# Two-layer hybrid trunk on one core: matmuls of one contraction depth issued together, exponentials one group ahead of their transposes, first weights on two queues

## The chip, the core and the metric

The kernel runs on one core of a Trainium2 chip. The core has five engines that run side by side and meet through semaphores: TensorE (PE, matmuls and transposes), VectorE (DVE), ScalarE (ACT, functions and casts), GpSimd (POOL) and SyncE (SP, which here issues DMAs). The time is that of the device in microseconds (us) for one execution; lower is better.

## What is computed

The reference is a trunk of two layers over 512 tokens of 1024 features, in float32. Each layer is a mixer, a residual layer norm, a convolutional FFN and a second residual layer norm:

```python
for layer in range(DEPTH):                    # DEPTH = 2
    mix = even_mixer(h, ...) if layer % 2 == 0 else odd_mixer(h, ...)
    h = layer_norm(DEEPNORM_ALPHA * h + mix, ...)
    ffn = conv_ffn(h, ...)
    h = layer_norm(DEEPNORM_ALPHA * h + ffn, ...)

def even_mixer(x, ...):                       # x @ w_in, split
    o_a = gated_delta_rule(q_a, k_a, v_a, g, beta)   # 6 heads of 128
    o_a = rms_norm(o_a, norm_w) * silu(z_a)
    o_b = dilated_attention(q_b, k_b, v_b, rel_bias) # 3 groups x 4 heads of 64
    return concatenate([o_a, o_b]) @ w_out

def dilated_branch(q, k, v, window, dilation, rel_bias):  # once per group
    s = where(mask, q . k * dh ** -0.5 + bias, -inf)      # blocks of 128 queries
    m = max(s); p = exp(s - m); l = sum(p)
    return (p / l) @ v, m + log(l)            # groups are joined by softmax over these
...
def gla_chunked(q, k, v, log_a):              # odd mixer, 4 heads, key 64, value 128
    o_n = (q_n * exp(b_n)) @ state + attn @ v_n
    state = exp(b_last) * state + (k_n * exp(b_last - b_n)).T @ v_n
```

The odd mixer joins differential attention (4 heads) with this gated linear attention (GLA).

## The kernel before

Activations lie as features by tokens: 8 tiles `h` of 128 x 512 for the trunk. The large products take float32 operands apart into a rounded part and a remainder (`xh` and `xl` of the activations, `wh` and `wl` of the weights), and each 128 x 128 block of weights becomes three products of 128 x 512 (`xh,wh`, `xl,wh`, `xh,wl`). A unit of weights is a tile `wr` of 128 x 1024 (512 KB, DMA from SP), cast to `wh` on ACT, with the remainder `wl` taken on DVE; one unit gives one output tile `pd` of 24 products. The small products of the mixers run in plain float32; in the trace each of these has two records.

The order on PE is written by a planner in the program. Every part of a mixer is a generator (a `Chain`), and `tile_of` polls the chains after each three products of a unit. A chain that yields `FREE` may go on as soon as PE has done its last piece, one that yields 0 waits for the estimated end plus a hop. So small products land between the products of a unit at places that the estimates set.

`swa_pair` does the dilated attention for a pair of heads, in two calls. For each of three groups g and both heads hh, the four blocks n of 128 queries give scores `sps` (group 0: 128-row products through `scores`; groups 1 and 2: plain products of 64 rows, since a head has 64 features), DVE adds the bias and takes the maxima (`mx`). The maxima are joined over the groups (`combine` into `mrow`), transposed into `pmx`, negated into `negm`, and 24 exponentials follow on ACT with sums `ls`. Then, group by group, PE transposes the exponentials (`pt`), DVE and ACT copy them out, and value products of 64 columns gather in `po`. While this runs, the units of the gate z of the gated delta rule (GDN) pass through PE; their tiles `pd` get a silu on ACT (`zs` or `h`). The GDN means (`pm`) get a logarithm and an exponential on ACT. `out_proj` ends the mixer.

`gla_pair` does two GLA heads. The output tile `po` of a head takes four 128-row products of the chunk's own attention (`vt,ga`) and three 64-row products with the state (`gs,qe`), which alternate.

At the start `START` names the order of the first loads: pieces of the trunk `x` (issued on SP) and of the first two weight units (issued on ACT, the first narrow unit feeds the gates, tile `pa`). ACT casts and DVE subtracts in the same order. `par` and `con` are tables of parameters and constants. `gates` computes the decay of GDN in a chain over ACT and DVE that ends in a scan; `pg` is PE's transpose behind it.

Of the kernel before, what the change touches and what calls it, by code (L numbers as in the profile page):

```python
# [9 lines left out]
F32 = mybir.dt.float32  # L10
# [3 lines left out]
ALU = mybir.AluOpType  # L14
# [3 lines left out]
P = 128  # L18
S = 512
# [5 lines left out]
NCH = S // P  # L25
# [9 lines left out]
_NP = 0  # L35
# [23 lines left out]
for _n, _w in (("ident", 128), ("maskT", 128), ("nm1", 32), ("i32", 32), ("lm", 4 * 32), ("scan", 512),  # L59
# [30 lines left out]
EVEN_SEQ = "h0 h1 h2 h3 h4 h5 q00 v0 q01 v1 q02 v2 q10 q11 q12 z0 z1 z2 z3 z4 z5"  # L90
ODD_SEQ = "0D12G3abcd"

START = (("x", 0, 1), (0, 0, 4), ("x", 1, 2), (1, 0, 2), ("x", 2, 3), (1, 2, 5), ("x", 3, 4), (0, 4, 8), ("x", 4, 5),
         ("x", 5, 6), (1, 5, 8), ("x", 6, 7), ("x", 7, 8))
WARM = 8
LEAD = 3
AHEAD = 2
# [14 lines left out]
FREE = -1  # L112
# [53 lines left out]
class Scratch:  # L166


    def __init__(self, t, pool, n, more=None):
        self.t, self.pool, self.free, self.of = t, pool, list(range(n)), {}  # L170
        if more is not None:
            self.free += [(k, more) for k in range(more.shape[1])]

# [21 lines left out]
class Trunk:  # L195
# [14 lines left out]
    def setup(self):  # L210
        nc, tc, ctx = self.nc, self.tc, self.ctx
# [9 lines left out]

        self.ones = keep.tile([P, P], F32, name="ones")
        nc.gpsimd.memset(self.ones, 1.0 / P)
        idle = keep.tile([P, 1], F32, name="idle")
        tc.keep_in_program_order(nc.scalar.copy(out=idle, in_=self.ones[:, 0:1]))
        for what, a, e in START:
            if what == "x":
                nc.sync.dma_start(self.h[:, a, :], self.xt[:, a, :])
            else:

                u, w = first[what]
                n = 64 if u in NARROW else P
                tc.keep_in_program_order(nc.scalar.dma_start(w[0][:, a * n : e * n], self.wts[u][:, a * n : e * n]))
        self.par = keep.tile([P, _NP], F32, name="par")
        self.con = keep.tile([P, _NCC], F32, name="con")

        warm = self.sps("warm")
# [4 lines left out]
        self.onesP, self.onesK = (keep.tile([P, P], F32R, name=f"ones{i}") for i in "PK")  # L242
        for x, n in ((self.onesP, P), (self.onesK, 512)):
            nc.vector.tensor_scalar(out=x, in0=self.ones, scalar1=P / n, scalar2=None, op0=ALU.mult)
        self.cst = keep.tile([P, 3], F32, name="cst")
        self.one, self.lneps, self.gdneps = (self.cst[:, i : i + 1] for i in range(3))
        nc.gpsimd.memset(self.one, 1.0)
        nc.gpsimd.memset(self.lneps, LN_EPS)
# [503 lines left out]
    def even(self):  # L752
# [8 lines left out]
        def t1(n, w, bufs):  # L761
            return mp.tile([P, w], F32, name=self.nm(n), tag=n, bufs=bufs)

        self.enter(EVEN)
        g = {"zero": t1("zero", 1, 1)}
        seq = EVEN_SEQ.split()
# [480 lines left out]
    def swa_pair(self, pair, taken, vts, bg, o, mp, t1):  # L1247
# [12 lines left out]
        for g in range(3):  # L1260
            while len(taken) < 2 * g + 2 or X.room() < 5 or not self.bias:
                yield None
            q, k = taken[2 * g : 2 * g + 2]
            for hh in range(2):
                r = slice(64 * hh, 64 * hh + 64)
                hd = 2 * pair + hh
                tiles = []
                for n in range(NCH):
                    w = 256 if g == 0 and n > 0 else P
                    if n == 0 or (g == 0 and n == 2):  # L1270
                        while X.room() < 1:
                            yield None
                        x = X.get("sc")
                        held.append(x)
                        off = 0
                    dst = x[:, off : off + w]
                    off += w
                    bias = bg[0][:, hd, 256 - w : 256] if g == 0 else bg[g][:, hd, :]
                    k0 = n * P + P - w
                    ps = self.sps("sps")  # L1280
                    if g == 0:
                        m = max(0, 256 - w)
                        self.scores(ps[:, : w + m], q, k, hh, slice(n * P, (n + 1) * P), slice(k0, k0 + w + m))
                    else:
                        T.matmul(ps[:, :w], lhsT=q[r, n * P : (n + 1) * P], rhs=k[r, k0 : k0 + w], start=True, stop=True)
                    ci = hh * 12 + g * NCH + n
                    V.tensor_tensor_reduce(out=dst, in0=ps[:, :w], in1=bias, scale=0.125, scalar=-3e38,
                                           op0=ALU.add, op1=ALU.max, accum_out=mx[:, ci : ci + 1])
                    tiles.append((dst, k0, w))
                    yield FREE  # L1290
                sc[g, hh] = tiles
            X.put(*(q + k[0] + k[1] if g == 0 else [q, k]))

        def rows(cols, rw):

            pr = self.sps("rows")
            T.transpose(out=pr[0:24, 0:P], in_=cols, identity=self.ident)
            tr = t1("tr", P, 2)
            V.tensor_copy(out=tr[0:24, :], in_=pr[0:24, 0:P])
            for hh in range(2):  # L1300
                G.dma_start(rw[hh : hh + 1, :], tr[12 * hh : 12 * hh + 12, :])
            yield 2500
# [11 lines left out]
        combine(rw, ALU.max, mrow)  # L1314
        yield 0
        pm = self.sps("pmx")
        for g in range(3):
            for n in range(NCH):
                src = perm(mrow[0:2, :])[:, n, :] if g else mrow[0:2, n * P : (n + 1) * P]
                T.transpose(out=pm[:, (g * NCH + n) * 2 : (g * NCH + n) * 2 + 2], in_=src, identity=self.ident[0:2, 0:2])  # L1320
        X.put(mrow)
        nm = t1("negm", 24, 2)
        V.tensor_scalar(out=nm, in0=pm[:, 0:24], scalar1=-1.0, scalar2=None, op0=ALU.mult)
        ls = t1("ls", 24, 2)
        for g in range(3):
            for hh in range(2):
                for n in range(NCH):
                    ci = (g * NCH + n) * 2 + hh
                    li = hh * 12 + g * NCH + n
                    dst, k0, w = sc[g, hh][n]  # L1330
                    A.activation(out=dst, in_=dst, func=AF.Exp, bias=nm[:, ci : ci + 1], accum_out=ls[:, li : li + 1])
                yield 0 if g == 0 and hh == 1 else FREE
        po = self.sps("po")
        for g in range(3):
            while len(vts[g]) < 2:
                yield None
            pts = {}
# [19 lines left out]
            for n in range(NCH):  # L1357
                for i in range(len(pts[0, n])):
                    for hh in range(2):
# [4 lines left out]
                        else:  # L1364
# [1 line left out]
                        vt, f = (vts[g][pair], kb * P) if g else (vts[g][kb // 2], kb % 2 * HS + P * pair)  # L1366
                        T.matmul(dst, lhsT=vt[:, f + 64 * hh : f + 64 * hh + 64], rhs=src,
                                 start=(g == 0 and n == 0 and i == 0), stop=(g == 2 and n == NCH - 1))
                yield FREE
            X.put(*temps)  # L1370
        X.put(*held)
        if pair:
# [172 lines left out]
    def gla_pair(self, pr, cs, qk, vts, gm, o, t1, done):  # L1545
# [4 lines left out]
        def ch(x, n):  # L1550
            return x[:, n * P : (n + 1) * P]
# [100 lines left out]
        vt = vts["G"]  # L1652
# [15 lines left out]
        yield 0  # L1668
        for hh in range(2):
            po = self.sps("po")  # L1670
            for n in range(NCH):
                if n:
                    T.matmul(ch(po, n), lhsT=qe[rr[hh], n * P : (n + 1) * P], rhs=sts[n][rr[hh]], start=True, stop=False)
                T.matmul(ch(po, n), lhsT=ch(ats[hh], n), rhs=ch(vt[n], 2 * pr + hh), start=(n == 0), stop=True)
            ss = t1("gss", NCH, 4)
            for n in range(NCH):
                A.activation(out=ch(ats[hh], n), in_=ch(po, n), func=AF.Square, accum_out=ss[:, n : n + 1])
            yield 0
            yield from self.norm_out(po, ss, o, 4 + 2 * pr + hh, self.p("lnorm"), t1)
            done.append(2 * pr + hh)  # L1680
# [322 lines left out]
```

## Time and profile before

| | |
|---|---|
| median of 3 runs | 1410.34 us (1410.32 to 1410.57) |
| the profiled execution | 1412.89 us |
| its span | 1411.1 us |
| granted PE clock over the span | 0.996 of full |
| PE busy | 1385.7 us, 98% |
| DVE, ACT, POOL busy | 839.3, 673.5, 179.8 us |
| stretches of the span | start to 18 us; even mixer to 374; out_proj and norm to 440 |

The profiled execution took 1.79 us beyond its span and lies 2.55 us above the median. PE has work in nearly all of the span, so a change counts by what it does to PE's own time or to the few waits of PE. A busy PE isn't a PE at its peak: matmuls are pipelined, and the length of a record overlaps with the next. What one product costs is therefore read from the start of one record to the start of the next.

### The profile page before, as it was taken

What the parts mean: (1) busy time and instruction counts of PE and PEld (TensorE: products, weight loads), DVE (VectorE), ACT (ScalarE), POOL (GpSimd) and SP (SyncE); (2) the same over time, 40 slices, a digit from 0 to 9 for tenths busy, and PEclk for the clock granted to TensorE, in tenths of its full rate; (3) what the DMA queues carried; (4) which work ended last, traced back from release to release, by engine and by line L of the source; (5) the groups of instructions that cost most, each with busy time, mean ns of one, the idle gap of its engine ahead of it and who ended that gap; (6) DMA issues with size and microseconds to landing.
All of it is one profiled execution on the core that took longest, in us unless ns stands there. A gap on an engine that the chain in (4) does not pass through costs nothing.

```text
span 1411.1 us, 22721 instructions
## 1 busy us (share of the span) xinstructions
PE 1385.7 (98%) x9050; PEld 1151.2 (82%) x9050; DVE 839.3 (59%) x1635; ACT 673.5 (48%) x1285; POOL 179.8 (13%) x237
## 2 busy tenths in 40 slices
PE   8999999999999999999999999999999999999997
PEld 6878787777798888888888977878898888888886
DVE  6876744544586555555243797777776555553354
ACT  6644433644857344434132755557565344432133
POOL 2103012011023111111010310000131111110010
PEclk9999999999999999999999999999999999999998
DMA  7434112121342322323233313211303322223221
GB/s 248 144 111 149 47 61 75 36 73 61 98 128 76 99 95 97 98 95 100 96 98 98 88 61 105 75 46 60 120 31 119 99 96 95 99 95 100 91 73 60
DMA packets 41457, 130.42 MB, mean 92 GB/s; under 512 B 4637, under 2 KB 9485, under 8 KB 41352
## 3 DMA queue, kind: packets, MB, share of 16 engines
q1 hardware_dynamic: 35584, 119.05, 26.1%
q10 hardware_dynamic: 4184, 4.92, 1.2%
q0 software_dynamic: 1584, 5.00, 1.1%
q8 instruction: 71, 1.16, 0.3%
q14 instruction: 34, 0.28, 0.1%
HBM read 126.76 MB, written 5.29 MB: 94 GB/s over the span
## 4 chain that ended last, share of the span: by engine, by line
PE 83%; DVE 6%; ACT 5%; DMA 3%; issue 2%; POOL 1%; ACTq 0%; DVEq 0%; POOLq 0%
PE pd L487 18%; PE pd L488 18%; PE pd L489 17%; PE pd L371 16%; PE pd L397 3%; DMA wr<-wts 2%; PE pc L159 1%; PE po L159 1%; PE sps L159 1%; PE pz L159 1%; PE py L159 1%; PE pa L159 1%; PE dsc L159 1%; DVE wl L159 1%; PE dpo L159 1%
## 5 line engine op out<-in xcount | busy, mean ns | idle before, releaser
L500 DVE TENSOR_TENSOR wl<-wr,wh 128x1024 fp32r<-128x1024 f32 (+1 forms) x153 | 187.9, 1229 | 301.8 <-ACT wh L499 298.7
L488 PE MATMUL pd<-xl,wh 128*128 128x512 f32 (+1 forms) x968 | 353.6, 366 | 0.2 <-DVE xl L684 0.2
L487 PE MATMUL pd<-xh,wh 128*128 128x512 f32 (+1 forms) x968 | 353.1, 366 | 0.4 <-ACT xh L683 0.4
L489 PE MATMUL pd<-xh,wl 128*128 128x512 f32 (+1 forms) x968 | 353.1, 365 | 0.0
L499 ACT CAST wh<-wr 128x1024 fp32r<-128x1024 f32 (+1 forms) x156 | 159.8, 1030 | 196.7 <-PE pd L488 171.4
L487 PEld LDWEIGHTS pd<-xh,wh 128*128 128x128 f32 x968 | 182.4, 189 | 30.4 <-ACT xh L683 0.9
L488 PEld LDWEIGHTS pd<-xl,wh 128*128 128x128 f32 x968 | 182.6, 189 | 30.1 <-DVE xl L684 1.1
L489 PEld LDWEIGHTS pd<-xh,wl 128*128 128x128 f32 x968 | 182.7, 189 | 29.5 <-issue 0.8
L371 PE MATMUL pd<-xh,wh 128*128 128x512 f32 x424 | 172.7, 407 | 0.0
L371 PE MATMUL pd<-xl,wh 128*128 128x512 f32 x424 | 170.9, 403 | 0.0
L487 PE MATMUL pd<-ah,wh 128*128 128x512 f32 (+1 forms) x396 | 145.1, 366 | 0.0
L489 PE MATMUL pd<-ah,wl 128*128 128x512 f32 (+1 forms) x396 | 144.7, 366 | 0.0
L488 PE MATMUL pd<-al,wh 128*128 128x512 f32 (+1 forms) x396 | 144.7, 365 | 0.0
L721 DVE SCALAR_TENSOR_TENSOR y<-pd,par,y 128x510 f32<-128x510 f32 (+1 forms) x176 | 130.4, 745 | 2.8
L371 PE MATMUL pd<-xh,wl 128*128 128x512 f32 x424 | 117.8, 402 | 0.0
L730 POOL TENSOR_TENSOR al<-y,ah 128x512 fp32r<-128x512 f32 x44 | 59.1, 1343 | 407.6 <-ACT ah L729 407.6
L159 DVE TENSOR_TENSOR wl<-wr,wh 128x1024 fp32r<-128x1024 f32 x63 | 77.1, 1224 | 42.6 <-PE pd L371 17.6
L159 ACT CAST wh<-wr 128x1024 fp32r<-128x1024 f32 x63 | 65.9, 1047 | 66.6 <-PE pd L371 48.2
L371 PEld LDWEIGHTS pd<-xl,wh 128*128 128x128 f32 x424 | 80.5, 190 | 16.2 <-issue 1.9
L371 PEld LDWEIGHTS pd<-xh,wh 128*128 128x128 f32 x424 | 80.4, 190 | 15.7 <-issue 0.3
L371 PEld LDWEIGHTS pd<-xh,wl 128*128 128x128 f32 x424 | 76.4, 188 | 14.6 <-issue 0.7
L487 PEld LDWEIGHTS pd<-ah,wh 128*128 128x128 f32 x396 | 74.7, 189 | 12.2
(387 smaller groups left out, 1868.6 us busy)
## 6 DMA issues: line engine op xcount, KB each, us to landing
wr<-wts SPq DMA_DIRECT2D x213, 512.0 KB, 3.4
h<-xt SPq DMA_DIRECT2D x16, 256.0 KB, 4.1
rep<-tab POOLq DMA_DIRECT2D x1, 3072.0 KB, 15.5
h<-gd POOLq DMA_DIRECT2D x6, 256.0 KB, 7.5
qe<-ge ACTq DMA_DIRECT2D x5, 256.0 KB, 4.4
bd<-rep ACTq DMA_DIRECT2D x1, 1024.0 KB
out<-h SPq DMA_DIRECT2D x2, 512.0 KB, 3.2
con<-con SPq DMA_DIRECT2D x1, 544.0 KB
```

Source lines behind the costliest of these rows:

```text
L159: r = fn(*a, **k)
L371: self.nc.tensor.matmul(ps, lhsT=w[part][:, k * P : (k + 1) * P], rhs=x[:, k, :], start=(i == 0), stop=(i == 23))
L397: self.nc.tensor.matmul(pss[b][:, a : a + n], lhsT=chunk(x[:, k, :], c), rhs=ws, start=(k == 0 and a == 0 and not part and x is self.xh), ...
L487: nc.tensor.matmul(ps, lhsT=wh, rhs=ah, start=first, stop=False)
L488: nc.tensor.matmul(ps, lhsT=wh, rhs=al, start=False, stop=False)
L489: nc.tensor.matmul(ps, lhsT=wl, rhs=ah, start=False, stop=last)
L499: A.copy(out=hi, in_=raw)
L500: V.tensor_tensor(out=lo, in0=raw, in1=hi.bitcast(F32), op=ALU.subtract)
L721: V.scalar_tensor_tensor(out=y[:, sft:], in0=ps[:, : S - sft], scalar=w(2 - sft), in1=y[:, sft:], op0=ALU.mult, op1=ALU.add)
L730: G.tensor_tensor(out=al[:, f, :], in0=y, in1=ah[:, f, :].bitcast(F32), op=ALU.subtract)
```

## The change

It has six parts. Scores of groups 1 and 2 take one tile `ps4` for four products, issued together. Only the maxima of two groups are transposed, since groups 1 and 2 share one maximum (`pmx` 8 products a pair in place of 12). The exponentials become a generator `exps(g)`: group g+1 is issued ahead of the transposes of group g, where before all three groups came ahead of all transposes. The value products of a group are issued without a yield between the blocks. GLA's three state products come ahead of the four others. `START` cuts the first weights into other pieces, of which three are issued on ACT and three on SP, between the pieces of x. Tiles are placed or widened so that all start at multiples of 128 bytes.

```diff
-START = (("x", 0, 1), (0, 0, 4), ("x", 1, 2), (1, 0, 2), ("x", 2, 3), (1, 2, 5), ("x", 3, 4), (0, 4, 8), ("x", 4, 5),
-         ("x", 5, 6), (1, 5, 8), ("x", 6, 7), ("x", 7, 8))
+START = (("x", 0, 1), (0, 0, 2), ("x", 1, 2), (1, 0, 2), ("x", 2, 3), (0, 2, 5), ("x", 3, 4), (1, 2, 5), ("x", 4, 5),
+         (0, 5, 8), ("x", 5, 6), (1, 5, 8), ("x", 6, 7), ("x", 7, 8))
+FIRST = 3
...
+        for i in range(n):
+            pool.tile([P, S], F32, name=t.nm("x"), tag=f"x{i}", bufs=1)
...
-        for what, a, e in START:
+        for i, (what, a, e) in enumerate(START):
...
-                tc.keep_in_program_order(nc.scalar.dma_start(w[0][:, a * n : e * n], self.wts[u][:, a * n : e * n]))
-        self.par = keep.tile([P, _NP], F32, name="par")
+                here = i < 2 * FIRST
+                d = (nc.scalar if here else nc.sync).dma_start(w[0][:, a * n : e * n], self.wts[u][:, a * n : e * n])
+                if here:
+                    tc.keep_in_program_order(d)
+        self.par = keep.tile([P, -(-_NP // 32) * 32], F32, name="par")[:, :_NP]
...
+                if g:
+
+                    ps4 = self.sps("sps")
+                    for n in range(NCH):
+                        b = slice(n * P, (n + 1) * P)
+                        T.matmul(ps4[:, b], lhsT=q[r, b], rhs=k[r, b], start=True, stop=True)
                 for n in range(NCH):
...
-                        T.matmul(ps[:, :w], lhsT=q[r, n * P : (n + 1) * P], rhs=k[r, k0 : k0 + w], start=True, stop=True)
+                        ps = ps4[:, n * P : (n + 1) * P]
...
-        for g in range(3):
+        for g in range(2):
             for n in range(NCH):
                 src = perm(mrow[0:2, :])[:, n, :] if g else mrow[0:2, n * P : (n + 1) * P]
...
-        for g in range(3):
+
+        def exps(g):
             for hh in range(2):
                 for n in range(NCH):
-                    ci = (g * NCH + n) * 2 + hh
+                    ci = (min(g, 1) * NCH + n) * 2 + hh
...
+        yield from exps(0)
         po = self.sps("po")
         for g in range(3):
+            if g < 2:
+                yield from exps(g + 1)
...
-                yield FREE
+            yield FREE
             X.put(*temps)
...
+            for n in range(1, NCH):
+                T.matmul(ch(po, n), lhsT=qe[rr[hh], n * P : (n + 1) * P], rhs=sts[n][rr[hh]], start=(n == 1), stop=False)
             for n in range(NCH):
-                if n:
-                    T.matmul(ch(po, n), lhsT=qe[rr[hh], n * P : (n + 1) * P], rhs=sts[n][rr[hh]], start=True, stop=False)
-                T.matmul(ch(po, n), lhsT=ch(ats[hh], n), rhs=ch(vt[n], 2 * pr + hh), start=(n == 0), stop=True)
+                T.matmul(ch(po, n), lhsT=ch(ats[hh], n), rhs=ch(vt[n], 2 * pr + hh), start=False, stop=(n == NCH - 1))
```

The first list is PE in `swa_pair` of pair 1 before the change, from group 1 on (`sps` scores, `sq` queries and keys, `pd` a unit of the gate z).

```order
L159 MATMUL sps_3832<-sq_3586,sq_3512 128x128
L371 MATMUL pd_3825<-xl,wh_3666 128x512
L159 MATMUL sps_3835<-sq_3586,sq_3512 128x128
L371 MATMUL pd_3825<-xh,wh_3666 128x512
L159 MATMUL sps_3838<-sq_3586,sq_3512 128x128
L159 MATMUL sps_3841<-sq_3586,sq_3512 128x128
L159 MATMUL sps_3846<-sq_3586,sq_3512 128x128
L371 MATMUL pd_3825<-xl,wh_3666 128x512
L159 MATMUL sps_3852<-sq_3586,sq_3512 128x128
L159 MATMUL sps_3855<-sq_3586,sq_3512 128x128
L159 MATMUL sps_3858<-sq_3586,sq_3512 128x128
L371 MATMUL pd_3825<-xh,wh_3666 128x512
```

And PE at the same place with the change:

```order
L160 MATMUL sps_3893<-sq_3589,sq_3545 128x128 x4
L378 MATMUL pd_3832<-xh,wl_3690 128x512 x3
L160 MATMUL sps_3906<-sq_3589,sq_3545 128x128 x4
L160 MATMUL sps_3916<-sq_3754,sq_3682 128x128 x4
L378 MATMUL pd_3832<-xh,wl_3690 128x512 x3
L160 MATMUL sps_3930<-sq_3754,sq_3682 128x128 x4
L160 MATMUL pm_3940<-hi_3617,onesP 128x512
```

The eight score products of group 1 stood in runs of one to three with single weight products between; now the sixteen of groups 1 and 2 stand in runs of four, eight and four, with three weight products between two runs.

The next list is PE in `gla_pair`, first head, before (`dpo` is differential attention, `vt,ga` the chunk's attention, `gs,qe` the state).

```order
L159 MATMUL dpo_8817<-vt_8234,dat_8784 128x128
L159 MATMUL po_8824<-vt_8770,ga_7582 128x128
L159 MATMUL po_8824<-gs_8798,qe_7974 128x128
L159 MATMUL po_8824<-vt_8774,ga_7582 128x128
L159 MATMUL po_8824<-gs_8800,qe_7974 128x128
L159 MATMUL po_8824<-vt_8778,ga_7582 128x128
L159 MATMUL po_8824<-gs_8802,qe_7974 128x128
L159 MATMUL po_8824<-vt_8789,ga_7582 128x128
```

And with the change:

```order
L160 MATMUL dpo_8874<-vt_8291,dat_8841 128x128
L160 MATMUL po_8881<-gs_8855,qe_8031 128x128
L160 MATMUL po_8881<-gs_8857,qe_8031 128x128
L160 MATMUL po_8881<-gs_8859,qe_8031 128x128
L160 MATMUL po_8881<-vt_8827,ga_7639 128x128
L160 MATMUL po_8881<-vt_8831,ga_7639 128x128
L160 MATMUL po_8881<-vt_8835,ga_7639 128x128
L160 MATMUL po_8881<-vt_8846,ga_7639 128x128
```

The two kinds alternated from product to product; now the three state products stand together, ahead of the four others.

The last lists are ACT at the end of the even mixer, pair 1 (`sc` the scores of groups 1 and 2 that get their exponential, `pt` transposed exponentials, `zs` and `h<-pd` the silu of gate z), first before.

```order
L159 ACTIVATE sc_3831,ls_3994<-sc_3831,negm_3992 128x128 x4
L159 ACTIVATE sc_3845,ls_3994<-sc_3845,negm_3992 128x128 x4
L159 ACTIVATE sc_3861,ls_3994<-sc_3861,negm_3992 128x128 x4
L159 ACTIVATE sc_3877,ls_3994<-sc_3877,negm_3992 128x128 x4
L159 COPY pt_4080<-pt_4075 128x512
L159 COPY pt_4087<-pt_4083 128x384
L159 ACT_TABLE_LOAD
L159 ACTIVATE h<-pd_3971 128x512
L159 ACTIVATE h<-pd_4082 128x512
L159 ACTIVATE zs_4143<-pd_4118 128x512
L159 COPY h<-pt_4165 128x512
L159 COPY h<-pt_4187 128x512
```

And with the change, from the copies on:

```order
L160 COPY pt_4113<-pt_4108 128x512
L160 COPY pt_4123<-pt_4119 128x384
L160 ACT_TABLE_LOAD
L160 ACTIVATE zs_4118<-pd_4065 128x512
L160 ACT_TABLE_LOAD
L160 ACTIVATE sc_3921,ls_4045<-sc_3921,negm_4043 128x128 x4
L160 ACTIVATE sc_3935,ls_4045<-sc_3935,negm_4043 128x128 x4
L160 COPY h<-pt_4171 128x512
L160 ACT_TABLE_LOAD
L160 ACTIVATE h<-pd_4127 128x512
L160 COPY h<-pt_4202 128x512
L420 ACT_TABLE_LOAD
```

All sixteen exponentials of groups 1 and 2 stood together ahead of the copies; now the last eight stand behind the copies of group 0 and a silu, with a load of ACT's function table on either side.

## Rows read from the trace of the kernel before

**Rows 1.** Page of the profile, part 1: busy time, share of the span, instructions.

```profile
PE 1385.7 (98%) x9050; PEld 1151.2 (82%) x9050; DVE 839.3 (59%) x1635; ACT 673.5 (48%) x1285; POOL 179.8 (13%) x237
```

**Rows 2.** List of waits, PE: us in total, times, longest.

```profile
PE pg L159 <- ACT wh L159: 1.5, 1, 1.5
...
PE po L159 <- ACT pt L159: 1.3, 1, 1.3
```

**Rows 3.** Timeline of PE, plain weight products; columns: start, length, line, operation, count.

```profile
21.54 1.98 PE L371 MATMUL pd<-xh,wl 128*128 128x512 f32 x8
23.36 0.39 PE L371 MATMUL pd<-xh,wh 128*128 128x512 f32 x1
```

**Rows 4.** Timeline of PE, scores of pair 0, group 2; two records are one product.

```profile
242.73 0.48 PE L159 MATMUL sps<-sq,sq 64*128 64x128 f32 x2
243.15 1.20 PE L371 MATMUL pd<-xh,wl 128*128 128x512 f32 x4
244.28 0.48 PE L159 MATMUL sps<-sq,sq 64*128 64x128 f32 x2
```

**Rows 5.** Timeline of PE, scores of pair 0, group 1.

```profile
204.44 1.36 PE L159 MATMUL sps<-sq,sq 64*128 64x128 f32 x10
205.74 0.50 PE L371 MATMUL pd<-xl,wh 128*128 128x512 f32 x1
```

**Rows 6.** Timeline of PE, value and state products of one GLA head.

```profile
925.97 1.16 PE L159 MATMUL dpo<-vt,dat 128*128 128x128 f32 x8
926.97 0.39 PE L159 MATMUL po<-vt,ga 128*128 128x128 f32 x2
927.28 0.48 PE L159 MATMUL po<-gs,qe 64*128 64x128 f32 x2
...
929.37 0.71 PE L159 MATMUL po<-vt,ga 128*128 128x128 f32 x4
```

**Rows 7.** Timeline of PE, transposes of the maxima of pair 1.

```profile
346.77 1.36 PE L159 MATMUL pmx<-con,mrow 2*128 2x2 f32 x12
```

**Rows 8.** Timeline of ACT and of its DMA queue, start of the kernel.

```profile
4.01 1.36 ACTq L233 DMA_DIRECT2D wr<-wts  x2
5.42 0.62 ACT L257 CAST xh<-h 128x512 fp32r<-128x512 f32 x1 [3.19 <-DMA h<-xt]
```

**Rows 9.** Timeline of PE, first weight products.

```profile
7.16 0.79 PE L507 MATMUL pd<-xh,wh 128*128 128x512 f32 x1 [2.37 <-DVE wh L500]
```

**Rows 10.** Timeline of ACT, weight unit ahead of the gates.

```profile
17.30 1.05 ACT L159 CAST wh<-wr 128x1024 fp32r<-128x1024 f32 x1 [1.14 <-DMA wr<-wts]
```

**Rows 11.** Timeline of DVE, end of the gates' chain.

```profile
28.02 1.21 DVE L159 TENSOR_TENSOR_SCAN h<-con,h 6x512 f32<-6x512 f32 x1
```

**Rows 12.** Table by window, all engines; busy us (count), PEclk, DMA share, GB/s.

```profile
29.00:35.00 6.00, 5.66 (x20) 4.57 (x21) 3.77 (x8) 2.54 (x5) 3.25 (x6) 0.72 0.37 103
```

**Rows 13.** Timeline of ACT, end of the even mixer.

```profile
348.39 0.40 ACT L159 ACTIVATE h<-h,negm 128x128 f32<-128x128 f32 x1 [0.97 <-DVE negm L159]
...
352.71 1.28 ACT L413 ACT_TABLE_LOAD   x1
354.01 0.72 ACT L159 ACTIVATE dt<-dt,cst 128x512 f32<-128x512 f32 x1
...
360.83 0.39 ACT L159 ACTIVATE sc<-sc,negm 128x128 f32<-128x128 f32 x1
...
367.95 1.28 ACT L159 ACT_TABLE_LOAD   x1
...
373.26 2.18 ACT L683 CAST xh<-o 128x512 fp32r<-128x512 f32 x4
```

**Rows 14.** Timeline of PE, mean of GDN pair and first product of out_proj.

```profile
335.73 0.50 PE L159 MATMUL pm<-hi,onesP 128*128 128x512 f32 x1
...
373.93 0.50 PE L487 MATMUL pd<-xh,wh 128*128 128x512 f32 x1 [0.41 <-ACT xh L683]
```

More of the change, by code (lines that the diff above doesn't have):

```diff
@@ L223, in setup @@
         nc.gpsimd.memset(self.ones, 1.0 / P)
-        idle = keep.tile([P, 1], F32, name="idle")
-        tc.keep_in_program_order(nc.scalar.copy(out=idle, in_=self.ones[:, 0:1]))
-        for what, a, e in START:
+        self.cst = keep.tile([P, 32], F32, name="cst")
+        tc.keep_in_program_order(nc.scalar.copy(out=self.cst[:, 8:9], in_=self.ones[:, 0:1]))
+        for i, (what, a, e) in enumerate(START):
             if what == "x":
@@ L244, in setup @@
             nc.vector.tensor_scalar(out=x, in0=self.ones, scalar1=P / n, scalar2=None, op0=ALU.mult)
-        self.cst = keep.tile([P, 3], F32, name="cst")
         self.one, self.lneps, self.gdneps = (self.cst[:, i : i + 1] for i in range(3))
@@ L762, in t1 @@
             return mp.tile([P, w], F32, name=self.nm(n), tag=n, bufs=bufs)
+        for i in range(4):
+            t1(f"st{i}", P, 2)
         self.enter(EVEN)
@@ L1279, in swa_pair @@
                     k0 = n * P + P - w
-                    ps = self.sps("sps")
                     if g == 0:
+                        ps = self.sps("sps")
                         m = max(0, 256 - w)
@@ L1297, in rows @@
             T.transpose(out=pr[0:24, 0:P], in_=cols, identity=self.ident)
-            tr = t1("tr", P, 2)
+            tr = t1("tr", P, 1)
             V.tensor_copy(out=tr[0:24, :], in_=pr[0:24, 0:P])
@@ L1321, in swa_pair @@
         X.put(mrow)
-        nm = t1("negm", 24, 2)
-        V.tensor_scalar(out=nm, in0=pm[:, 0:24], scalar1=-1.0, scalar2=None, op0=ALU.mult)
+        nm = t1("negm", 16, 2)
+        V.tensor_scalar(out=nm, in0=pm[:, 0:16], scalar1=-1.0, scalar2=None, op0=ALU.mult)
         ls = t1("ls", 24, 2)
-        for g in range(3):
+        def exps(g):
             for hh in range(2):
                 for n in range(NCH):
-                    ci = (g * NCH + n) * 2 + hh
+                    ci = (min(g, 1) * NCH + n) * 2 + hh
                     li = hh * 12 + g * NCH + n
```

## The prediction

> **What bounds the kernel now.** I read the page's busy times first: PE is busy for 1385.7 us, 98% of the span [rows 1]. All that PE waits is 25 us, so a gain has to come from PE's own time or from one of its few long waits. The list of waits comes next. Two of them lie near the change: 1.5 us ahead of `pg`, behind the gates' chain, and 1.3 us ahead of `po`, behind ACT's copy `pt` at the end of the even mixer [rows 2]. Then the timeline of PE, where I read starts, not lengths: eight plain weight products start 23.36 - 21.54 = 1.82 us apart, 0.2275 each [rows 3]. That is the price of a product with nothing around it. FFN and out_proj run at that price, have no small products among them and are touched by none of the six parts.
>
> The small products cost more than their own time. Around a score of 64 rows, 242.73 to 244.28 is 1.55 us for one score and four weight products [rows 4]. The four would take 0.91. Five scores in a row, with the way out, take 205.74 - 204.44 = 1.30, or 0.26 each, some 0.22 without the way out [rows 5]. So a lone score brings 1.55 - 0.91 - 0.22 = 0.42 us that is neither work nor a wait: PE goes to another contraction depth and back. GLA shows it without weight products or another engine: six products that alternate between 128 and 64 rows start 929.37 - 926.97 = 2.40 apart, 0.40 each, while four of one depth just ahead take 926.97 - 925.97 = 1.00, 0.25 each [rows 6]. A turn is thus 0.15 to 0.21, a visit (there and back) 0.3 to 0.42.
>
> **Scores, maxima and values on PE.** Score visits fall from 15 to 5 by the order of the whole program, products unchanged: 10 x 0.42 = 4.2 less. Of the transposes of maxima 8 go (4 in each pair) at 1.36 / 12 = 0.11 [rows 7]: 0.9 less. Visits for value products fall from 11 to 8; no row prices these alone, so 0 to 3 x 0.42 = 1.3. Against that, the new order puts single transposes between weight products where before they stood in fours. Going through both orders pair of neighbours by pair of neighbours with the intervals of the rows gives 4.8 less up to out_proj, where the simple sum says 5.1 to 6.4. I take 4.8.
>
> **GLA.** Visits of state products fall from 12 to 4: 8 x 0.3 to 0.42 is 2.4 to 3.4; the neighbours give 3.5, since in the second and third heads weight products stood between. I take 3.4. The first product now needs all three states at once, where before it needed one; their last was done on DVE about when PE came to it, so 0 to 0.3 of wait, inside the half microsecond below.
>
> **Start.** Two of five weight issues leave ACT's queue. The last two took it from 4.01 to 5.37, and the first cast came at 5.42 [rows 8], the first weight product 1.74 later at 7.16 [rows 9]. If the issues held it, the cast can come up to 1.0 sooner; the view names the landing of x as releaser, and if that is all, nothing is gained. I take 0.3. Larger is what follows. The unit behind the first two lands late and holds ACT for 1.14 us [rows 10]; behind it on ACT stands the copy with which the gates begin, and at the end a scan on DVE from 28.02 to 29.23 [rows 11], then `pg`. With the change the unit is issued ahead of `par` and `con` (792 KB). I take the chain to end 1.5 to 2 us sooner, and PE's wait of 1.5 to fall to 0.3: 1.2 (0 to 1.5). Behind that wait the granted clock is 0.72 over 6 us [rows 12]: 0.56 of it, 3.4 us, at 1.2 GHz in place of 2.4, which costs 1.7. PE had stood idle just before; without the idling I take 1.5 of it back (0 to 1.7). What comes later in exchange, `par` and `con`, is first read at 19 us. Start: 3.0, from 0 to 4.
>
> **The end of the even mixer.** Here the saving on PE meets another bound. ACT runs without a gap from the exponentials of group 0 to the first cast for out_proj, 348.39 to 373.26 [rows 13], and PE waits 1.3 ahead of `po` and 0.41 ahead of out_proj at 373.93 [rows 14]. The change doesn't take work off this chain; it cuts it up. Group 2's exponentials stand behind a silu, and each turn between exponential and silu loads a table: from the copies of the mean to the first cast there are eight loads where 348.39 to 373.26 has three. The chain in the new order: the old 24.87; 5 loads at 1.30 (352.71 to 354.01 [rows 13]) 6.5; one more copy 0.6; one more silu 0.5; two casts of weights at 1.05 [rows 10] 2.1; the cast 0.6; hand-overs 0.7 as my estimate. Sum 35.9. In the order it starts behind the mean `pm`, 0.34 after its first product, which is at 335.73 before [rows 14] and by the neighbours' intervals 1.57 sooner (beside the start's gain), since the rest of the saving lies behind it. Out_proj can start at 335.73 - 1.57 + 0.34 + 35.9 = 370.4, against 373.93: 3.5 sooner, not the 4.8 that PE saves. So 1.3 goes back into waits ahead of the last transposes, the last copy and the first cast.
>
> The Trainium skill's page "ScalarE: Activation LUTs" speaks against this part: its Rules for kernel authors say to finish everything of one table set before going to another, and its section What ACT_TABLE_LOAD costs gives 1283 ns for a load and about 1380 more for a drain. The trace agrees with the load (1.28) and not with the drain: the next activation starts 0.02 us behind it [rows 13]. By the page's 2.66 the five loads would be 13.3 in place of 6.5.
>
> **Alignment and the rest.** Some tiles lie at multiples of 128 bytes already, those lent from `h`; an exponential of 128x128 there takes 0.40, on an own tile `sc` 0.39 [rows 13]. I take 0 for the alignment; a per cent of ACT's and DVE's work would be hidden by PE anyway, except on the chain just worked out, where it is 0.4. Small new waits of the other pair and of GLA: 0.5 (0 to 2).
>
> **Sum.** 3.5 + 3.4 + 3.0 - 0.5 = 9.4 less than the profiled execution's 1412.89, so 1403.5 there; that execution lies 2.55 above the median of 1410.34, so about 1401.0 as a median. A change of 0.2% (2.8 us) is about what can be told from none here: 1407.5 to 1413.2 is the same.
>
> **Rivals.**
> - *ACT takes more at the end of the mixer.* PE's idling there is split into three waits of about 1 us. If the clock falls behind them as at the start (1.7 [rows 12]) and two more hand-overs of 1.3 appear, 4.3 goes: 1405.3. For it: the fall at the start. Against it: the 1.3 ahead of `po` led to no slower products. Chance 0.20.
> - *The start gives nothing*: x on the SP queue lands later for the weights put between its pieces, and the gates' wait stays. 1401.0 + 3.0 = 1404.0. For it: the first cast waited for x [rows 8]. Against: the bytes are the same. Chance 0.14.
> - *The turns aren't PE's.* If the 0.42 is DVE holding the score tiles, grouping saves nothing; then 3.0 - 1.3 is left, 1408.6. Against: GLA's 0.40, where DVE has no part. Chance 0.04.
> - *A load of a table costs double*, what [rows 13] don't show: eight of them at 1.3 more are 10.4, 1411.4. By the page of the Trainium skill named above that is what a switch costs. Chance 0.02.
> - *ACT and PE in step (slower).* At the same place each silu needs the last product of a unit and each group's transposes need exponentials behind that silu. Where the unit's end and the transposes stand the wrong way round, a whole unit lies bare: 24 x 0.2275 = 5.5. One costs half the gain; two, 10.9, turn the sign; three give 1417.4. Against it: in the order the unit of the silu between groups 1 and 2 ends ahead of group 0's transposes. Chance 0.03.
>
> The forecast itself gets 0.57. **How the numbers follow.** Low end: the even mixer's 4.8 in full, its 2 us of waits gone too, GLA's 3.5 and the start's 3.5 make 13.8: 1396.5. High end: 4.8 and 3.4, without 1.3, 1.7 of clock and 1.7 of other waits, with nothing from the start, 3.5: 1406.8. Outside are the last three rivals, 0.09, and tails. Faster are forecast and the first two rivals, 0.91; the same the third and fourth, 0.06; slower the last, 0.03.
>
> **What would show it.** Right: scores start 0.22 apart in fours, and the seven products of a GLA head take about 1.9 in place of 2.7; `pg` waits under 0.5 and the clock in 29 to 35 us is 1.00; out_proj starts near 367.4 in the trace; ACT shows eight loads at the end of the mixer and PE three waits there. Wrong: a wait ahead of group 2's transposes of over 3 us, out_proj later than 370, a first weight product later than 7.2, or a longer FFN, which no step here moves.

## The result and the profile after

The changed kernel took 1418.05 us as a median (1417.31 to 1420.39, 4 runs), the kernel before 1410.45 beside it: a ratio of 1.0056, 95% interval 1.0039 to 1.0074. It is slower by 7.9 us (5.5 to 10.4) where 9.4 less were forecast. Its profiled execution has this head of the page:

```profile
span 1416.6 us, 22717 instructions
...
PE 1391.9 (98%) x9042; PEld 1148.4 (81%) x9042; DVE 838.1 (59%) x1636; ACT 681.0 (48%) x1291; POOL 179.6 (13%) x237
```

PE works 6.2 us longer than before [rows 1] with eight products fewer. What the prediction said of scores and GLA on PE is there. The timeline of PE in pair 0, group 2, shows the eight scores of both heads in a row (16 records), 1.63 us to the weight product behind them, 0.20 each:

```profile
239.50 1.71 PE L160 MATMUL sps<-sq,sq 64*128 64x128 f32 x16
241.13 0.50 PE L378 MATMUL pd<-xh,wh 128*128 128x512 f32 x1
```

Before, a lone score with the way there and back took 0.42 beyond itself [rows 4]. Two GLA heads, in the timeline of PE:

```profile
930.26 0.93 PE L160 MATMUL po<-gs,qe 64*128 64x128 f32 x6
931.12 1.16 PE L160 MATMUL po<-vt,ga 128*128 128x128 f32 x8
932.21 0.93 PE L160 MATMUL po<-gs,qe 64*128 64x128 f32 x6
933.07 1.16 PE L160 MATMUL po<-vt,ga 128*128 128x128 f32 x8
```

A head takes 932.21 - 930.26 = 1.95 us, where six of its seven products took 2.40 [rows 6]. So the time is lost elsewhere, and in work that counts as busy. The table by window (busy us and count for PE, PEld, DVE, ACT, POOL; clock; DMA) shows it: first the stretch behind `pg` and the end of the even mixer, then three stretches of the FFNs:

```profile
29.00:35.00 6.00, 6.00 (x20) 4.71 (x19) 3.37 (x5) 1.87 (x5) 3.44 (x7) 0.72 0.49 125
368.00:374.00 6.00, 4.96 (x30) 3.73 (x31) 4.28 (x8) 5.97 (x10) 0.90 (x2) 1.00 0.30 90
460.00:640.00 180.00, 180.00 (x776) 145.91 (x776) 97.02 (x113) 75.27 (x98) 21.50 (x17) 1.00 0.29 94
670.00:740.00 70.00, 70.00 (x311) 57.98 (x310) 27.02 (x29) 19.14 (x21) 6.82 (x5) 1.00 0.29 91
1080.00:1260.00 180.00, 180.00 (x776) 145.96 (x775) 96.36 (x113) 74.57 (x97) 20.72 (x16) 1.00 0.30 96
```

The same three stretches of the kernel before:

```profile
460.00:640.00 180.00, 180.00 (x796) 149.05 (x795) 100.19 (x117) 76.16 (x99) 21.99 (x17) 1.00 0.30 97
670.00:740.00 70.00, 70.00 (x310) 57.90 (x309) 27.63 (x29) 17.71 (x20) 5.51 (x4) 1.00 0.29 95
1080.00:1260.00 180.00, 180.00 (x796) 149.06 (x795) 99.71 (x116) 76.01 (x100) 20.71 (x16) 1.00 0.30 98
```

From 460 to 640 us both kernels do nothing on PE but the up projection of the first FFN: same matmuls, no wait, clock 1.00. Before, 796 start in 180 us; after, 776. That is 2.5% more time for each, or, from start to start, 226.7 ns before and 232.4 after (mean over the 1720 and 1679 pairs of full products that follow each other in 440 to 640 and 1070 to 1260 us). The other up projection (1080 to 1260) is the same. The down projection (670 to 740) is not: 310 and 311. The groups by line say which products these are: those that stream `xh` or `xl`, not those that stream `ah` or `al`. Their mean lengths, for `xl` and for `al`, were 390 and 389 ns before:

```profile
L488 PE MATMUL pd<-xl,wh 128*128 128x512 f32 x744 | 289.9, 390 | 0.2 <-DVE xl L684 0.2
...
L488 PE MATMUL pd<-al,wh 128*128 128x512 f32 x308 | 119.8, 389 | 0.0
```

With the change they are 395 and 389:

```profile
L495 PE MATMUL pd<-xl,wh 128*128 128x512 f32 x744 | 293.4, 395 | 0.0
...
L495 PE MATMUL pd<-al,wh 128*128 128x512 f32 x308 | 119.8, 389 | 0.0
```

Both kernels issue these products from the same statement of the source and in the same order. What differs is the address, as the built programs place the tiles: `xh` starts at byte 32896 of each partition in both, `wh` at 86400 before and at 86528 after, since tiles widened to multiples of 128 bytes stand between. The distance was 53504, an even multiple of 128 (209 x 256), and is now 53632, an odd one. The blocks of these tiles are multiples of 256 bytes apart, so this holds for every product. `ah` and `wh` moved together and are 32768 apart in both.

From the first layer-norm mean to the second, which encloses the first FFN, the trace has 362.2 us before and 367.2 after, for the second FFN 362.3 and 367.9. These 10.6 us exceed the whole loss; the rest of the kernel is 5.1 us shorter in the span. (Not every tile lies at a multiple of 128 bytes with the change: 94 of 1259 placements are still off one, 291 of 1262 were before.)

### The profile page after: what moved, and what is told of

Same layout as the page of the kernel before. It is cut to its first block, busy times and chain, and to the rows that moved or that the text cites. A ratio compares the mean times of both kernels' runs of the same rounds, so it can differ in the third digit from the quotient of the medians.

```text
span 1416.6 us, 22717 instructions
## 1 busy us (share of the span) xinstructions
PE 1391.9 (98%) x9042; PEld 1148.4 (81%) x9042; DVE 838.1 (59%) x1636; ACT 681.0 (48%) x1291; POOL 179.6 (13%) x237
## 4 chain that ended last, share of the span: by engine, by line
PE 85%; DVE 6%; ACT 3%; DMA 3%; issue 2%; POOL 1%; ACTq 0%; POOLq 0%; DVEq 0%
PE pd L494 18%; PE pd L495 18%; PE pd L496 18%; PE pd L378 17%; PE pd L404 3%; DMA wr<-wts 2%; PE pc L160 1%; PE pz L160 1%; PE po L160 1%; PE py L160 1%; DMA h<-xt 1%; PE dsc L160 1%; PE pa L160 1%; PE sps L160 1%; PE dpo L160 1%
## 5 line engine op out<-in xcount | busy, mean ns | idle before, releaser
L506 ACT CAST wh<-wr 128x1024 fp32r<-128x1024 f32 (+2 forms) x157 | 159.4, 1022 | 206.2 <-PE pd L495 183.7
L495 PEld LDWEIGHTS pd<-al,wh 128*128 128x128 f32 x396 | 74.7, 189 | 12.3
```

The source lines that it names most:

```text
L495: nc.tensor.matmul(ps, lhsT=wh, rhs=al, start=False, stop=False)
L506: A.copy(out=hi, in_=raw)
```

## The experiments

Three theories were tried against each other. **A**: a weight product is dear when the streamed operand and the weights aren't a multiple of 256 bytes apart. **B**: scratch tiles, now all at multiples of 128, collide with PE's reads. **C**: the weights' own place counts.

**e1, x moved.** The tile of 128 bytes is put ahead of `xh`, so weights and scratch stay where the change put them.

```diff
         self.h = keep.tile([P, KD, S], F32, name="h")
+        self.cst = keep.tile([P, 32], F32, name="cst")
         self.xh = keep.tile([P, KD, S], F32R, name="xh")
...
-        self.cst = keep.tile([P, 32], F32, name="cst")
```

> The changed kernel, with the 128-byte tile cst placed ahead of xh and xl in place of behind them. Only h's neighbours move: xh, xl and ones by 128 bytes; weights, scratch tiles, order and schedule stay. In the changed kernel xh and the weights wh lie an odd multiple of 128 bytes apart (53632), in the kernel before an even one (53504); here an even one again (53504). Theory A (the distance, modulo 256 bytes, between the streamed operand and the weights sets the price of a weight product): the products of the up projections start 226.7 ns apart again in place of 232.4, and the time falls by 12 us for the two up projections and 4 to 6 for the mixers and out_proj, to 1401 to 1403. Rival B (scratch tiles at multiples of 128 bytes collide with PE's reads): 232.4 stays, 1418. Rival C (the place of the weights alone): 232.4 stays, 1418.

Measured: ratio 0.9956 (0.9943 to 0.9968), 1405.24 against 1411.29 for the kernel before on the same chip. The table by window of e1:

```profile
29.00:35.00 6.00, 6.00 (x29) 4.95 (x28) 3.38 (x5) 3.13 (x6) 3.43 (x7) 1.00 0.56 184
368.00:374.00 6.00, 5.90 (x18) 4.47 (x19) 5.92 (x9) 5.07 (x9) 0.00 (x0) 0.72 0.16 46
460.00:640.00 180.00, 180.00 (x796) 149.08 (x795) 99.47 (x116) 76.29 (x100) 20.69 (x16) 1.00 0.30 97
670.00:740.00 70.00, 70.00 (x311) 57.97 (x310) 28.38 (x30) 19.02 (x21) 5.52 (x4) 1.00 0.29 92
```

The up projection is back at 796 in 180 us. Scratch and weights lie as in the changed kernel, so B and C fall. Against the changed kernel this is 1.0056 / 0.9956, about 1.0% or 14 us, for one tile's place. The time is 2 us above A's range of 1401 to 1403. Between the two traces the FFNs give back 10.9 us, near A's 12, but mixers and out_proj 2.2 where A had 4 to 6: in the mixers a weight product that follows another takes 228.6 ns in e1 and 232.3 in the changed kernel, so the price there is 3.7 ns and not 5.7.

**e2, weights moved in the kernel before.**

```diff
+        gap = keep.tile([P, 32], F32, name="gap")
         self.ones = keep.tile([P, P], F32, name="ones")
...
-            tr = t1("tr", P, 2)
+            tr = t1("tr", P, 1)
```

> The kernel before, with an unused tile of 128 bytes ahead of ones, which moves everything behind xl by 128 bytes, weights and scratch alike; room for it comes from tr with one buffer in place of two. Scratch tiles keep their odd places. A: xh and wh now lie 53632 apart, the up projections go to 232.4 ns for a product, down projections (ah and weights moved together) stay at 226.7; the time rises by 13 to 17 us to 1423 to 1428. B: nothing changes, 1410. C: as A.

Measured: ratio 1.0095 (1.0079 to 1.011), 1425.46. The table by window of e2:

```profile
460.00:640.00 180.00, 180.00 (x773) 144.81 (x772) 97.14 (x114) 73.96 (x96) 20.74 (x16) 1.00 0.30 95
670.00:740.00 70.00, 70.00 (x310) 57.92 (x309) 26.34 (x29) 18.76 (x21) 6.28 (x5) 1.00 0.28 90
```

With nothing of the change but the odd distance and the single buffer of `tr`, which the change has too, the up projection slows to 773 in 180 us (233.3 ns) and the down projection keeps its 310. So `xh`'s own place isn't the cause either: it is unmoved here. The size is at the middle of A's range.

**e3, xl alone moved.**

```diff
         self.xh = keep.tile([P, KD, S], F32R, name="xh")
+        self.cst = keep.tile([P, 32], F32, name="cst")
         self.xl = keep.tile([P, KD, S], F32R, name="xl")
...
-        self.cst = keep.tile([P, 32], F32, name="cst")
```

> The changed kernel, with cst between xh and xl: xl lies an even multiple of 128 bytes from the weights, xh an odd one. A: a product that streams xh takes 232.4 ns and one that streams xl 226.7, so the third of the products recovers, and the time is 1412 to 1414. B and C: 232.4 for all, 1418.

Measured: one run of 1410.32, below the 1412 to 1414 that A gave. The up projection in the table by window of e3:

```profile
460.00:640.00 180.00, 180.00 (x788) 147.50 (x787) 98.79 (x115) 74.94 (x99) 20.65 (x16) 1.00 0.30 97
```

788 in 180 us lies between 776 and 796, 228.9 ns on average. By position in the three it is 232.5 after a product `xh,wh`, 225.8 after `xl,wh` and 228.3 after `xh,wl`. A had 232.4 for both that stream `xh`; one of them pays only a quarter of the price. So the distance acts product by product, as A says, but A's price doesn't simply add up over them. Why is open.

**e4 and e11, x moved by 64 and by 32 bytes.**

```diff
+        gap = keep.tile([P, 16], F32, name="gap")
         self.xh = keep.tile([P, KD, S], F32R, name="xh")
...
-        self.cst = keep.tile([P, 32], F32, name="cst")
+        self.cst = keep.tile([P, 16], F32, name="cst")
```

e11 has 8 and 24 in place of 16 and 16.

> The changed kernel, with 64 bytes of cst's 128 ahead of xh, so that xh and xl lie 64 bytes off a multiple of 128 from the weights. A read strictly (anything but a multiple of 256 costs): 232 ns, 1418. A read with 128 as the one bad distance: 226.7 ns, 1401 to 1403. A with the cost growing with the distance: about 229.5 ns, 1410. B and C: 1418.

> The changed kernel with 32 bytes of cst ahead of xh: xh lies 96 bytes past a multiple of 256 from the weights. A read strictly: 232 to 233.5 ns for a product of the up projections, 1418. If only 64 and 128 are bad distances: 226.7 ns, 1402 to 1405.

Measured: 1417.95 and 1422.18, one run each. The up projection in the table by window of e4, then of e11:

```profile
460.00:640.00 180.00, 180.00 (x773) 145.04 (x772) 97.17 (x114) 73.91 (x96) 20.72 (x16) 1.00 0.29 94
```

```profile
460.00:640.00 180.00, 180.00 (x770) 144.72 (x769) 96.43 (x113) 73.98 (x97) 20.80 (x16) 1.00 0.28 94
```

With the distance 64 past a multiple of 256 it is 773 (233.3 ns), with 96 past it 770 (234.3), with 128 past it 776 (232.4). A holds when read strictly: each distance tried that isn't a multiple of 256 costs 2.5 to 3.4%, e11 somewhat more than was expected. A multiple of 128 has no merit of its own.

**e12, ah moved.** On e1, the down projections' operands are moved.

```diff
         with tc.tile_pool(name=f"ff{layer}", bufs=1) as fp:
+            gap = fp.tile([P, 32], F32, name=f"gap{layer}")
             ah = fp.tile([P, NF, S], F32R, name=f"ah{layer}")
```

> The kernel of e1 with an unused tile of 128 bytes ahead of ah in each FFN: the operands ah and al of the down projections lie an odd multiple of 128 bytes from the weights (21 of the 22 units; the last unit's tiles lie behind al and move along), xh stays at an even one. A: down projections at 232 ns in place of 226.7, up projections at 226.7; the time 5 us over e1, 1409 to 1410. If the price hangs on xh's own place or on what runs beside the up projections: 226.7 everywhere, 1404.

Measured: one run of 1412.44. The table by window of e12:

```profile
460.00:640.00 180.00, 180.00 (x795) 149.02 (x794) 99.46 (x116) 76.57 (x100) 20.75 (x16) 1.00 0.29 97
670.00:740.00 70.00, 70.00 (x302) 56.30 (x301) 27.14 (x30) 18.99 (x21) 5.53 (x4) 1.00 0.28 93
```

Now the down projection pays (302 in 70 us, 233.3 ns) and the up projection doesn't. The price can be put on either by one unused tile. It goes with the pair of operands, not with a tile or with what else runs in that stretch. The time is 7 over e1, where 5 were expected and one run can't split the difference.

**e5 to e8, one part each taken back from e1**: e5 runs `exps(0)` to `exps(2)` ahead of the loop over the transposes; e6 has a tile and a yield for each score; e7 alternates GLA's products; e8 has the old `START` with all first weights on ACT. In short:

```diff
 e5
-        yield from exps(0)
+        for g in range(3):
+            yield from exps(g)
...
-            if g < 2:
-                yield from exps(g + 1)
 e6
-                    ps4 = self.sps("sps")
...
-                        ps = ps4[:, n * P : (n + 1) * P]
+                        ps = self.sps("sps")
+                        T.matmul(ps[:, :w], lhsT=q[r, n * P : (n + 1) * P], rhs=k[r, k0 : k0 + w], start=True, stop=True)
 e7
-            for n in range(1, NCH):
-                T.matmul(ch(po, n), lhsT=qe[rr[hh], n * P : (n + 1) * P], rhs=sts[n][rr[hh]], start=(n == 1), stop=False)
             for n in range(NCH):
+                if n:
+                    T.matmul(ch(po, n), lhsT=qe[rr[hh], n * P : (n + 1) * P], rhs=sts[n][rr[hh]], start=True, stop=False)
...
 e8
...
-FIRST = 3
+FIRST = 99
```

> The kernel of e1 (changed, x moved by 128 bytes), with all exponentials ahead of the transposes again. The prediction's step: issuing them a group ahead gives 1.3 us of PE's saving back to ACT's loads, and in e1 the waits there were followed by 1.6 us at the lower clock. If so, this kernel is 1 to 3 us faster than e1 (ratio to before 0.9935 to 0.995, e1 had 0.9956). Rival: the exponentials a group ahead feed PE sooner; then this one is slower than e1 by 1 us or more (over 0.9963).

> The kernel of e1, with the scores of groups 1 and 2 in a tile each and a yield between them, as before the change. The prediction's step: ten visits less at 0.42 us, so this one is 3 to 5 us slower than e1 (ratio to before 0.998 to 0.999). Rival (the turns are DVE's, or the gain is lost behind ACT at the end of the mixer): no difference from e1, 0.9956.

> The kernel of e1, with the GLA products alternating again. The prediction's step: eight visits less, 3.4 us; so this one is 3 to 3.8 us slower than e1 (ratio to before 0.998), and a head takes 2.7 us in place of 1.9. Rival (the saving is waited away behind): within 1 us of e1.

> The kernel of e1, with START as before and all first weights on ACT's queue. The prediction's step: the start gives 3.0 us, of which the first weight product is 0.7 and the wait ahead of pg 0.6 sooner or shorter in e1, and the clock did not fall there; so this one is 1.3 to 3 us slower than e1 (ratio 0.9965 to 0.9977). Rival (what the start gives is waited for later): within 0.7 us of e1.

| kernel | ratio to before | 95% interval | against e1, with the interval that the two give together |
|---|---|---|---|
| e1 | 0.9956 | 0.9943 to 0.9968 | |
| e5, exponentials together | 0.9954 | 0.9941 to 0.9966 | -0.3 us (-2.8 to 2.2) |
| e6, scores apart | 0.9982 | 0.9973 to 0.9990 | +3.7 us (1.5 to 5.8) |
| e7, GLA alternating | 0.9987 | 0.9978 to 0.9996 | +4.4 us (2.2 to 6.6) |
| e8, start as before | 0.9956 | 0.9942 to 0.9970 | 0.0 us (-2.7 to 2.7) |

The last column is the difference of the ratios times 1411. The two groupings are worth something on the order of what the turns said, and their rivals fall. e6 tests less than was meant: by the order of its trace the scores come in 11 visits, where the kernel before has 15 and e1 has 5, so it takes back six visits, 2.5 us at 0.42, and not ten. For e7 the traces can be read by stage: from the mean behind the first FFN to the mean of the second out_proj e7 takes 250.7 us and the kernel before 251.0, while the other kernels here with GLA grouped and `xh` at an even distance (e1, e5, e6, e8, e9, e10, e12) take 247.5 to 249.3, so 1.5 to 3.3 less than e7, where the prediction had 3.4.

e5 and e8 show no difference, but 2 us either way lie inside their intervals. Two views show how a gain can get lost. In e5 PE waits, by the list of waits, 1 us longer than before ahead of `po` [rows 2]:

```profile
PE po L160 <- ACT pt L160: 2.3, 1, 2.3
```

In e1 three waits ahead of the last value products and of out_proj take 1.5 in all. The clock falls at the end of the mixer in both: in e1 it is 0.72 from 368 to 374 us (above), in e5 0.58 from 360 to 366. The table by window of e5:

```profile
360.00:366.00 6.00, 4.06 (x32) 3.73 (x33) 0.69 (x1) 5.14 (x14) 0.00 (x0) 0.58 0.13 39
```

In e8 the timeline of PE shows

```profile
7.23 0.79 PE L514 MATMUL pd<-xh,wh 128*128 128x512 f32 x1 [2.44 <-DVE wh L507]
...
28.25 0.41 PE L160 MATMUL pg<-con,h 38*128 38x38 f32 x4 [0.31 <-issue]
```

and in e1

```profile
6.50 0.79 PE L514 MATMUL pd<-xh,wh 128*128 128x512 f32 x1 [1.72 <-DVE wh L507]
...
27.97 0.41 PE L160 MATMUL pg<-con,h 38*128 38x38 f32 x4 [0.86 <-ACT wh L160]
```

so in e8 the first weight product comes 0.7 later, but `pg` only 0.3 later, with a shorter wait. In these two executions, what PE gains at the front it mostly waits away ahead of `pg`.

**e9, the change without its alignment**, and **e10, with the start and the exponentials as before too.** e9 removes the preallocated tiles and the widening; e10 takes back e5's and e8's parts on top.

```diff
-        for i in range(n):
-            pool.tile([P, S], F32, name=t.nm("x"), tag=f"x{i}", bufs=1)
...
-        self.cst = keep.tile([P, 32], F32, name="cst")
+        idle = keep.tile([P, 1], F32, name="idle")
...
-        self.par = keep.tile([P, -(-_NP // 32) * 32], F32, name="par")[:, :_NP]
+        self.par = keep.tile([P, _NP], F32, name="par")
```

> The changed kernel without its sixth part: tiles lie as before the change, scratch at odd places, xh and the weights 53504 bytes apart; the other five parts stay. A: plain weight products take 226.7 ns and the time is that of e1 (ratio to before 0.9945 to 0.9965). If scratch at multiples of 128 bytes had a worth of its own, this kernel would be slower than e1 (over 0.997); if it had a price of its own, faster (under 0.9945).

> The kernel of e9, with the start and the order of the exponentials as before the change, so that grouping (scores, values, GLA) and the fewer transposes of maxima are left. By e5 and e8 neither of the two parts taken back moves the time: ratio 0.994 to 0.9965. If they support each other (start and exponentials both needed), it is over 0.997.

Measured: e9 0.9967 (0.9955 to 0.9979), e10 0.9944 (0.9932 to 0.9957). e9 has 226.7 ns again, with the scratch at odd places; it lies between the bounds set for it, and its interval overlaps e1's, so no worth of aligned scratch is shown, nor excluded up to 4 us or so. e10 is the fastest of all, 1403.65 against 1411.44; grouping and fewer transposes alone give 0.56% (0.43 to 0.68), and e1's interval overlaps it. e9 and e10, run beside each other, differ in the start and the order of the exponentials alone, and e10 is 3.2 us faster (0.8 to 5.7). So these two parts together gain nothing there, they cost; which of them, no run shows. The page of e10:

```profile
span 1401.2 us, 22709 instructions
...
PE 1374.5 (98%) x9042; PEld 1147.5 (82%) x9042; DVE 838.0 (60%) x1635; ACT 674.6 (48%) x1286; POOL 180.0 (13%) x237
```

PE's busy time is 11.2 us under that of before [rows 1], with a product rate in the FFN as before.

## Why the prediction was wrong

**The step that failed** is "I take 0 for the alignment", and with it the sentence that FFN and out_proj "are touched by none of the six parts". The prediction asked whether an operation is quicker on an aligned tile, looked at one operand at a time (0.40 against 0.39 for an exponential [rows 13]), and found rightly that it isn't. It didn't ask what else moves when a tile is widened: the distance between tiles that it leaves alone. The longest work of the kernel, weight products at 0.2275 [rows 3], hangs on that distance. The price was 14 us (changed kernel against e1). Between these two traces it is 13.1, of which the FFNs show 10.9, and the mixers and out_proj, whose weight products stream `xh` and `xl` too, 2.2. No rival had it, and the range ended at 1406.8. The prediction did name a longer FFN as a sign of being wrong, and that is the sign which came; out_proj later than 370 came too, by 0.13.

Without that price the sum was still 3 us too high: e1 gains 6.2 us (4.5 to 8.0) of the 9.4. Without the start's 3.0 the sum is 6.4.

**Grouping** was right. A visit of a score has about the price that it was given, as far as e6 can tell: 3.7 us (1.5 to 5.8) for six visits, where 0.42 each is 2.5. No run takes back all ten. GLA: 3.4 forecast, 4.4 (2.2 to 6.6) by time from e7 and 1.5 to 3.3 by stage; a head takes 1.95 us where 1.9 was said. That the grouped parts give the whole (e10: 7.9 us, 6.1 to 9.6) fits the 4.8 and 3.4 of the sum.

**The start** was mis-sized: 3.0 forecast, 0.0 (-2.7 to 2.7) from e8. The first weight product does come sooner (6.18 against 7.16 [rows 9]) and `pg` too (27.89, 1.45 sooner than the 29.34 of the kernel before), but PE still waits 1.56 ahead of `pg`:

```profile
6.18 0.50 PE L514 MATMUL pd<-xh,wh 128*128 128x512 f32 x1 [1.39 <-DVE wh L507]
...
27.89 0.41 PE L160 MATMUL pg<-con,h 38*128 38x38 f32 x4 [1.56 <-ACT wh L160]
```

So the chain moved up by about as much as PE did, the wait stayed, and the clock fell behind it as before, 0.72 from 29 to 35 us [rows 12] in the table above. The step behind this was to take the wait of 1.5 and the fall, read from one execution, as what the old start costs every time. The other runs show neither. With the old start the timelines show a wait ahead of `pg` of 0.31 in e8, of 0.69 in e10 and none in e2. With the new one they show 0.86 in e1, 0.53 in e12, 1.41 in e6 and none in e5, and these four are the same program up to `pg`. The clock in 29 to 35 us is below 1.00 in three of the fourteen traces: before, with the change and in e9. In e6 it is 1.00 behind a wait nearly as long as that of the kernel before; timeline of PE and table by window of e6:

```profile
28.00 0.41 PE L160 MATMUL pg<-con,h 38*128 38x38 f32 x4 [1.41 <-ACT wh L160]
```

```profile
29.00:35.00 6.00, 6.00 (x28) 4.96 (x27) 3.37 (x5) 3.09 (x6) 3.44 (x7) 1.00 0.59 175
```

**The end of the mixer** came out in its mechanism. The timeline of ACT shows the casts starting at 369.46 and, from the copy of the mean at 334.27, eight table loads, four of which are among these rows:

```profile
334.27 0.59 ACT L160 COPY dt<-pm 128x512 f32<-128x512 f32 x1 [1.15 <-PE pm L160]
...
349.30 1.28 ACT L160 ACT_TABLE_LOAD   x1
...
360.80 1.28 ACT L160 ACT_TABLE_LOAD   x1
...
365.78 1.28 ACT L160 ACT_TABLE_LOAD   x1
...
368.16 1.28 ACT L420 ACT_TABLE_LOAD   x1
369.46 3.75 ACT L690 CAST xh<-o 128x512 fp32r<-128x512 f32 x7
```

The chain took 369.46 + 0.6 - 334.27 = 35.8 us, where 35.9 was worked out. PE waits three times at its end, and out_proj starts at 370.13, in e1 at 368.10, where 367.4 was said. Timeline of PE with the change, then its last line in e1:

```profile
367.48 0.43 PE L160 MATMUL po<-h,vt 128*64 128x128 f32 x2 [0.37 <-DVE h L160]
368.20 1.09 PE L160 MATMUL po<-h,vt 128*64 128x128 f32 x14 [0.28 <-ACT h L160]
370.13 0.72 PE L494 MATMUL pd<-xh,wh 128*128 128x512 f32 x2 [0.84 <-ACT xh L690]
```

```profile
368.10 0.96 PE L494 MATMUL pd<-xh,wh 128*128 128x512 f32 x2 [0.84 <-ACT xh L690]
```

The loads cost 1.28 each, and behind seven of the eight the next activation starts 0.01 to 0.02 later (behind the fourth ACT waits 0.54 for DVE's `negm`). So the rival of a doubled load falls. The Trainium skill's page "ScalarE: Activation LUTs" (What ACT_TABLE_LOAD costs) adds a drain for a switch, about as long as the load; this trace doesn't show it. Whether the new order was worth its 1.3 us is open: e5 with the old order is no slower (-0.3 us), and e10 against e9 speaks against the new order or the new start.

**The clock rival** showed in e1's trace: the clock is 0.72 from 368 to 374 us behind those waits, which costs some 1.7 us (half speed for 0.56 of 6 us), and out_proj's head start of 5.8 us over before (368.10 against 373.93 [rows 14]) shrinks to 3.4 at the first mean (412.16 and 415.52 in the traces). In the changed kernel the same three waits were followed by clock 1.00.

## What to carry to other kernels

Before widening or aligning a tile, list the addresses of the operands that the longest-running matmuls stream and load, and keep their distance a multiple of 256 bytes, as here; then compare the count of matmuls per window in a stretch that the change should not touch. Products of another contraction depth belong together on PE: 0.3 to 0.4 us for each visit, and what the runs gave back fits that within their noise. Time gained ahead of a wait is only worth what the thing waited for gains as well. Before a single wait or a fall of the clock goes into a sum, look at a second execution: here both came and went among programs that begin alike.

## What was not expected of the hardware

A product of 128x512 with one operand streamed and the next weights loaded takes 226.7 ns when the two operands' start addresses in SBUF differ by a multiple of 256 bytes (32768, 37120 and 53504 among those tried) and 232.4 to 234.3 when they differ by 64, 96 or 128 more. It does so whether ACT or DVE is casting weights at that moment or not (232.4 for the 892 pairs without such work at the time and 232.3 for the 787 with it, in the changed kernel's two up projections). That the collision is between the streaming read and the load of weights is argued from this, not shown: no run here separates the two reads, and e3's 228.3 isn't explained by it. The Trainium skill's page "SBUF — State Buffer" (Who interferes with whom) gives PE two independent read ports, one for the streamed operand and one for weights, and lets only the ports shared by DVE and GpSimd contend; by that rule no distance would matter, and the 776 against 796 products in 180 us differ from it. Whether it is the same for other operand types or sizes was not tried.

The clock falls aren't a fixed price of a wait: behind 1.51 us ahead of `pg` it fell in the kernel before, and behind 1.41 in e6 it didn't; behind waits of 0.37, 0.28 and 0.84 it fell in e1 and not in the changed kernel. Nor does the program alone set their place. e1, e7 and e12 have the same even mixer at the same addresses, and in their one trace each the clock fell in e1 from 368 us on, in e12 in 349 to 355 and in e7 in 75 to 81, here by the table by window of e12, then of e7:

```profile
349.00:355.00 6.00, 6.00 (x24) 4.75 (x25) 2.55 (x5) 5.47 (x25) 0.00 (x0) 0.72 0.48 133
```

```profile
75.00:81.00 6.00, 6.00 (x118) 4.55 (x107) 5.43 (x22) 1.05 (x1) 0.00 (x0) 0.72 0.32 90
```

What decides it, no run here shows.
